# Thirty-one turns for thirty-two experts: which expert gets a turn is read from a table while the kernel runs

## The chip, the cores and the metric

The kernel runs on one core of one Trainium2 chip. The metric is the device time of one execution in microseconds (us), taken as the median of several runs. The core's engines work side by side, each through its own list of instructions: PE (matrix products), DVE (elementwise work and reductions), ACT (ScalarE), POOL (GpSimd) and SP (SyncE, which here issues most of the DMA transfers).

## The reference

The input x has 256 tokens of 1024 numbers. Everything is float32. Three layers follow one another:

- a block with a gated causal convolution over the tokens, a projection, and a residual;
- an expert layer: a router picks for each token one of 4 groups and in it the best 2 of 8 experts, and each token's row goes through its two experts;
- a multi-head latent attention layer and a block-wise attention layer, each with a gate, an output projection and a layer norm.

The expert layer is what matters here. With h the normalised tokens:

```
grp    = argmax(h @ w_rg + b_rg)                      # one of 4 groups
v, i   = top_k((h @ w_re + b_re)[grp's 8 experts], 2)
gate   = softmax(group logits)[grp] * softmax(v)
expert = grp * 8 + i                                  # 2 of 32 experts per token
out[token] += gate * (silu(xb @ w_gate[e]) * (xb @ w_up[e])) @ w_down[e]
```

An expert's three weights are 1024x512, 1024x512 and 512x1024: 2.097 MB each.

## The kernel before

**The weights** come as 2 MB pieces in one fixed list, made by `pieces()` (lines 83 to 131): the convolution block's, then three for each of the 32 experts (part 0 gate, part 1 up, part 2 down), then those of the attention layers. For the experts the list goes gate e+1, up e+1, down e, so a turn's down weight comes behind the next turn's first two. Class `Weights` (line 137) issues them on SP in this order, up to 12 pieces ahead of the one in use, into a fixed rotation of buffers: `ring_a` and `ring_b` with three each, and during the expert stage four more (`c`, `d`, `d`, `f`) in memory that earlier tiles have left. SP waits at each piece until the buffer's last reader is done. Every piece has its source address in the program. The pieces of the attention layers use `ring_a` alone.

**Routing** (lines 715 to 773). DVE makes `oh1`, a 0/1 table of tokens by experts, and `G`, the gates. PE counts with a triangular matrix how many earlier tokens chose the same expert (`pp`), and DVE makes `posp` from it: the token's place with its expert, from 1, or 0. Then the pools of this part close (`ctxB.close()`), and the tiles of the expert stage take their memory.

**An expert's turn** (lines 971 to 1035). A turn holds 64 tokens (`CAP`). `group(e)` makes 0/1 matrices (`oh`) for four experts from `posp`, and `gather` multiplies the tokens, split into two rounded halves, by them: `xg`. `start` multiplies `xg` by the gate and the up weight, `hidden` and `hidden_t` make and transpose the hidden rows, and `proj_out` multiplies them by the down weight (`pys`). DVE weights the result (`yt`, line 1029), and `split` (lines 281 to 283) makes two halves `y`. Turns go in pairs: an even turn fills rows 0 to 63 of `y`'s first 512 columns and rows 64 to 127 of its second, an odd turn the other way round, so that one product per half, `scatter`, brings a pair's rows back to their tokens in four PSUM accumulators (`acc`). `scatter_matrix` makes the pair's matrix at its even turn from `oh` and `ig`, a tile with an identity and `G`. `put()` scatters the pair before at the next even turn. The turn before the last (`e == E - 2`) makes the last turn's hidden rows ahead, between the two halves of its own projection. The last pair is scattered behind the loop (lines 1127 to 1129), where the norm's squares follow (line 1142).

**An expert with more than 64 tokens** is finished at turn 20 (`OVF_AT`), under a condition on the largest place, `mxi`, that all engines read into a register: a loop over all 32 experts (`overflow`, line 886) with the places 65 to 256 in three rounds, each with its own loads of the weights.

The planner of the framework lays out each engine's list by the program's order and by when it expects things to be ready; from the end of the convolution to the end of the experts the products stay in the program's order (`pe_order`, line 194).

Of the kernel before, what the change touches and what calls it, by code (L numbers as in the profile page):

```python
# [13 lines left out]
P = 128  # L14
# [3 lines left out]
KD = 8  # L18
E = 32
FH = 512  # L20
CAP = 64
# [61 lines left out]
def pieces():  # L83

    out = []

    def add(shape, *key):
        out.append((key, shape))

    def add_ada(v):  # L90
        for h in range(2):
            add((KD, 512), "ada", v * D + h * 512)

    add_ada(1)
    add_ada(0)
    for q in range(4):
        add((KD, 512), "cwi", 256 * q)
    for v in (4, 3, 2):
        add_ada(v)
    wo_at = len(out)  # L100
    add((KD, 512), "cwo", 0)
    add_ada(5)
    add((KD, 512), "cwo", 512)
    moe_from = len(out)

    def add_moe(e, part):
        add(((KD, FH), (KD, FH), (4, D))[part], "moe", e, part)

    for e in range(E):
        if e == 0:  # L110
            add_moe(e, 0)
            add_moe(e, 1)
        if e + 1 < E:
            add_moe(e + 1, 0)
            add_moe(e + 1, 1)
        add_moe(e, 2)
    moe_to = len(out)
    add((KD, KVL + RD), "mwi", QL)
    for h in range(2):
        add((KD, 384), "mwi", 384 * h)  # L120
    add((2, 2048), "ukv", 0)
    for i in range(4):
        add((6, 384), "uq", 384 * i)
        if i % 2 == 0:
            add((KD, 512), "mwi", QL + KVL + RD + 256 * i)
    for h in range(2):
        add((KD, 512), "mwo", 512 * h)
    for w, a in (("bkv", D), ("bkv", 0), ("bkv", 512), ("bkv", D + 512), ("bwi", 0), ("bwi", D), ("bwi", 512),
                 ("bwi", D + 512), ("bwo", 0), ("bwo", 512)):
        add((KD, 512), w, a)  # L130
    return out, wo_at, moe_from, moe_to
# [5 lines left out]
class Weights:  # L137
# [14 lines left out]
    def fill(self, upto):  # L152
        while self.nload < min(upto, self.cap, len(self.src)):
            ap, shape, pool = self.src[self.nload]
            n = 1
            for s in shape:
# [27 lines left out]
def build(tc, A, out, dbg=None, stop=None):  # L184
# [34 lines left out]
    W = Weights(nc, order, 2 * (RING_A + RING_B))  # L219

    flat, at = A["wst"], 0
    for i, (key, shape) in enumerate(PIECES):
        n = 1
        for z in shape:
            n *= z
        if key[0] == "moe":
            if key[1:] == RING_D_AT:
                ring_d_from = len(W.src)
                W.pools[:0] = ["d"] * RING_D + ["f"]
            src = A["moe"][key[1], key[2]]  # L230
        else:
            if key == ("cwo", 512):
                W.cap = len(W.src)
                W.pools.insert(0, "c")
            src = flat[at:at + P * n].rearrange("(p n) -> p n", p=P)
            at += P * n
        W.add(src, shape, ring_a if i >= MOE_TO else None)
# [9 lines left out]
    cstp = pre.tile([P, C_N - C_SEL], F32, name="cstp")  # L247
    vec = const.tile([P, V_ROWS], F32, name="vec")
    x2 = pre.tile([P, NT, D], F32, name="x2")
# [19 lines left out]
    nc.vector.memset(zeros, 0.0)  # L269
    aff = const.tile([P, 4, KD], F32, name="aff")  # L270
    small = const.tile([P, 16], F32, name="small")
# [66 lines left out]
    nc.tensor.transpose(pv, vraw, ident)  # L338
    nc.vector.tensor_copy(vec, pv)
    nc.scalar.activation(small[:, 0:8], vec[:, V_C:V_C + 8], AF.Sigmoid)  # L340
    nc.vector.tensor_mul(small[:, 0:8], small[:, 0:8], vec[:, V_C:V_C + 8])
# [376 lines left out]
    dump("lg", lg)  # L718
    posp = rt.tile([P, NT, E], F32, name="posp")
    G = rt.tile([P, NT, E], F32, name="G")  # L720
    r1 = pre.tile([P, NT, 16], F32, name="r1")
# [43 lines left out]
    nc.vector.tensor_add(oh1, oh1, oh2)  # L765
    pp = psA.tile([P, NT, E], F32, name="pp", tag="adc")
    mm(pp[:, 0, :], tri, oh1[:, 0, :], True, True)
    mm(pp[:, 1, :], ones, oh1[:, 0, :], True, False)
    mm(pp[:, 1, :], tri, oh1[:, 1, :], False, True)
    nc.vector.scalar_tensor_tensor(posp, pp, 1.0, oh1, op0=OP.add, op1=OP.mult)  # L770
    rest_of_rows(1)
    dump("posp", posp)
    dump("G", G)
# [112 lines left out]
    def overflow():  # L886

        with tc.For_i(0, E, 1) as e:
            pc = mo.tile([P, NT], F32, name="pc", tag="pc")
            gc = mo.tile([P, NT], F32, name="gc", tag="gc")  # L890
# [4 lines left out]
            def part(n, k, c=0):  # L895
                wt = mo.tile([P, 512], F32, name="wo", tag="yh1")
                q = (D * k + c) if n == 2 else 512 * k
                nc.gpsimd.dma_start(wt, A["moe"][bass.ds(e, 1), n, :, q:q + 512].rearrange("o p n -> p (o n)"))
                return wt

            so = mo.tile([P, CAP], F32, name="so", tag="so")
            xg = mo.tile([P, KD, CAP], F32, name="xgo", tag="yl0")
            for r in range(1, T // CAP):
                nc.vector.tensor_scalar(so, slot64, float(CAP * r), None, op0=OP.add)
# [45 lines left out]
    for q in range(4):  # L950
        gather(*nxt, range(2 * q, 2 * q + 2), 4 * CAP, acc[q // 2][q % 2])

    ig = mo.tile([P, P + 4 * E], F32R, name="ig")
    nc.scalar.copy(ig[:, 2 * E:2 * E + P], ident)
# [15 lines left out]

    for e in range(E):
        if e == OVF_AT:
            put()
        if e == OVF_AT:
            W.cap = 1 << 30
            rv = nc.values_load(mxi[0:1, 0:1], min_val=0, max_val=T)
            with tc.If(rv > CAP):
# [17 lines left out]
        if hn is None:  # L995
            hid = hidden(pgu)
            pgu = None
        if e + 1 < E:
            pgu = pme.tile([P, 512], F32, name="pgu", tag="pgu")
# [3 lines left out]
        if e == 1:  # L1003
            most_slots(mxi)
        wu = W.get() if e + 1 < E else None
        if e % 2 == 0:
            if e != OVF_AT and e:
                put()
            se, gs = scatter_matrix(oh, e)
            start(e + 1, xg, 1, pgu, wu)  # L1010
            if e % 4 == 2 and e + 2 < E:
                del oh, xg
                oh, xg = group(e + 2)
                for q in range(4):
                    gather(oh, xg, range(2 * q, 2 * q + 2), 4 * CAP)
            y = [[mo.tile([P, 512], F32R, name=f"y{q}{j}", tag=f"y{q}{j}") for q in "hl"] for j in range(2)]
        elif wu is not None:
            start(e + 1, xg, 1, pgu, wu)
        del wu
        w = W.get()  # L1020
        if e == E - 2:
            hid = hidden(pgu)
        pys = proj_out(hT, e % 2, lambda c, o: w[:, c, o:o + 512], ahead if e == E - 2 else None)
        hT = w = None
# [7 lines left out]
        del pys, yt  # L1032
        if e % 2:
            done = (se, y)
            del se, y, gs
# [384 lines left out]
    xh, xl = big("xh", F32R), big("xl", F32R)  # L1420
    to_channels((0, 1), x2, vec[:, V_FIN:V_FIN + 8], None, xh, xl)
    fg = rows(A["final_g"].unsqueeze(0))
# [23 lines left out]
    def latent_q(i):  # L1446
        pq = chunk_t(KD, xh, xl)
        a, v = scaled_split(cqh[:, i, :], cql[:, i, :], pq, vec[:, V_QN + i:V_QN + i + 1])
        nc.scalar.activation(sqq[:, i, :], pq, AF.Square)
# [8 lines left out]
    for k in range(2):  # L1458
        pt = ps.tile([P, T], F32, name="ptc", tag="pt", bufs=2)
        for t in range(NT):  # L1460
            nc.tensor.transpose(pt[:, P * t:P * t + P], ckn[:, t, P * k:P * k + P], ident)
        scaled_split(ckh[:, k, :], ckl[:, k, :], pt, vec[:, V_KN + k:V_KN + k + 1])

# [250 lines left out]
```

## Time and profile before

| | |
|---|---|
| median of 3 runs | 935.23 us (932.19 to 936.95) |
| the profiled execution, its own time | 931.65 us |
| its span, from the first instruction to the last | 930.0 us |
| PE busy | 871.4 us, 94% of the span |
| DVE busy | 516.4 us, 56% |
| ACT busy | 362.2 us, 39% |
| mean granted TensorE clock | 0.986 |
| bytes moved by DMA | 289.44 MB, mean 311 GB/s |

Shares of busy time are means over stages with different limits, and a busy PE is one with a product under way, at whatever rate. The stages in the order of time: convolution block to about 170 us, routing to about 187, experts to about 629, attention layers to the end.

### The profile page before, as it was taken

How to read it: one execution, taken by the hardware profiler on the slowest of the kernel's cores; microseconds unless marked ns; L12 is line 12 of the kernel's file. 1: busy time of each engine (PE TensorE's matmuls, PEld its weight loads, DVE VectorE, ACT ScalarE, POOL GpSimd, SP SyncE). 2: the span in 40 equal slices, each digit the busy share in tenths (PEclk: the TensorE clock that was granted, in tenths of full speed). 3: DMA queues.
4: the chain of work that ended last, by engine and by line, in shares of the span. 5: the costliest groups of instructions: out<-in, count | busy, mean ns of one | idle time of the engine just before them, and what ended most of it. 6: DMA issues, size and time to landing. Idle time of an engine off the chain costs nothing. (4 is left out here: it accounts for less than half of the span.)

```text
span 930.0 us, 15479 instructions
## 1 busy us (share of the span) xinstructions
PE 871.4 (94%) x6249; PEld 611.3 (66%) x6249; DVE 516.4 (56%) x1255; ACT 362.2 (39%) x794; POOL 39.7 (4%) x50
## 2 busy tenths in 40 slices
PE   4899889899999999999799999789999999999996
PEld 1598456666555565656365565448998876988975
DVE  2699876523334333433223343247778867868876
ACT  1445555522112121212112121127776646545761
POOL 0000010000000000000000000001110000210112
PEclk9899999999999999999989999999999999999999
DMA  9995887799999999999999999995433423624211
GB/s 370 411 397 205 337 351 292 295 375 426 427 425 427 427 425 428 426 427 426 427 425 427 426 427 427 427 395 206 164 139 123 181 101 137 261 91 182 91 47 45
DMA packets 23580, 289.44 MB, mean 311 GB/s; under 512 B 2736, under 2 KB 3408, under 8 KB 6096
## 3 DMA queue, kind: packets, MB, share of 16 engines
q1 hardware_dynamic: 21872, 282.29, 73.4%
q10 hardware_dynamic: 1632, 6.11, 1.9%
q8 instruction: 51, 0.84, 0.4%
q14 instruction: 25, 0.20, 0.1%
HBM read 287.34 MB, written 1.05 MB: 310 GB/s over the span
## 5 line engine op out<-in xcount | busy, mean ns | idle before, releaser
L195 PE MATMUL pgu<-w,xg 128*64 128x256 f32 x2048 | 233.5, 381 | 4.0 <-DMA w<-in_moe 4.0
L195 PEld LDWEIGHTS pgu<-w,xg 128*64 128x64 f32 x2048 | 145.7, 137 | 89.9 <-issue 20.7
L195 PE MATMUL pys<-w,hTe 128*64 128x512 f32 x512 | 116.1, 595 | 5.4 <-DMA w<-in_moe 2.6
L283 DVE TENSOR_TENSOR sl<-w,sh 128x1024 fp32r<-128x1024 f32 (+2 forms) x82 | 95.6, 1173 | 18.8 <-ACT sh L282 17.7
L282 ACT CAST sh<-w 128x1024 fp32r<-128x1024 f32 (+2 forms) x82 | 81.3, 998 | 51.1 <-PE pj L195 47.5
L1029 DVE SCALAR_TENSOR_TENSOR yt<-pys,gs,g2b 64x512 f32<-64x512 f32 x64 | 48.0, 750 | 87.2 <-PE pys L195 86.1
L282 ACT CAST yh<-yt 64x512 fp32r<-64x512 f32 x64 | 39.5, 616 | 138.8 <-DVE yt L1029 134.7
L195 PE MATMUL pj<-xh,sh 128*128 128x256 f32 x304 | 86.6, 285 | 0.0
L195 PE MATMUL pj<-xl,sh 128*128 128x256 f32 x304 | 85.6, 282 | 0.0
L195 PE MATMUL pj<-xh,sl 128*128 128x256 f32 x304 | 85.4, 281 | 0.0
L195 PEld LDWEIGHTS pys<-w,hTe 128*64 128x64 f32 x512 | 36.2, 137 | 66.0 <-issue 54.5
L863 DVE TENSOR_TENSOR hid<-pgu,hid 128x256 f32<-128x256 f32 x32 | 13.6, 424 | 98.6 <-ACT hid L862 98.6
L862 ACT ACTIVATE hid<-pgu 128x256 f32<-128x256 f32 x32 | 12.3, 383 | 120.9 <-PE pgu L195 114.8
L195 PEld LDWEIGHTS pj<-xl,sh 128*128 128x128 f32 x304 | 57.1, 188 | 1.8 <-issue 1.7
L195 PEld LDWEIGHTS pj<-xh,sh 128*128 128x128 f32 x304 | 57.1, 188 | 1.7 <-issue 1.6
L195 PEld LDWEIGHTS pj<-xh,sl 128*128 128x128 f32 x304 | 57.1, 188 | 0.8 <-issue 0.8
L414 DVE SCALAR_TENSOR_TENSOR y<-up,wdw,y 128x256 f32<-128x256 f32 x120 | 52.5, 484 | 0.1
L283 DVE TENSOR_TENSOR yl<-yt,yh 64x512 fp32r<-64x512 f32 x64 | 43.9, 686 | 2.0
L282 ACT CAST wh<-w 128x512 fp32r<-128x512 f32 x48 | 29.1, 619 | 28.9 <-PE pu L195 21.3
L195 PE MATMUL pu<-hh,wh 128*128 128x256 f32 x128 | 36.7, 287 | 2.7 <-ACT wh L282 2.7
L283 DVE TENSOR_TENSOR wl<-w,wh 128x512 fp32r<-128x512 f32 x48 | 32.3, 684 | 11.9 <-ACT wh L282 11.1
L871 DVE COPY hTe<-pth 128x256 f32<-128x256 f32 x32 | 13.6, 424 | 43.5 <-PE pth L201 38.8
(344 smaller groups left out, 1565.4 us busy)
## 6 DMA issues: line engine op xcount, KB each, us to landing
w<-in_moe SPq DMA_DIRECT2D x95, 2048.0 KB, 32.1
w<-in_wst SPq DMA_DIRECT2D x32, 2048.0 KB, 9.0
w<-in_wst SPq DMA_DIRECT2D x5, 1152.0 KB, 5.1
w<-in_wst SPq DMA_DIRECT2D x2, 1536.0 KB, 11.1
wb<-in_wbd ACTq DMA_DIRECT2D x4, 512.0 KB, 6.8
w<-in_wst SPq DMA_DIRECT2D x2, 1024.0 KB, 22.4
w<-in_moe SPq DMA_DIRECT2D x4, 512.0 KB, 31.4
x<-in_x SPq DMA_DIRECT2D x1, 1024.0 KB, 11.4
```

Source lines behind the costliest of these rows:

```text
L195: ins = nc.tensor.matmul(o, l, r, start=start, stop=stop)
L282: a = nc.scalar.copy(hi, src)
L283: return a, (eng or nc.vector).tensor_sub(lo, src, hi.bitcast(F32))
L414: nc.vector.scalar_tensor_tensor(y[:, m, :], u, wdw[:, m, k:k + 1], y[:, m, :], op0=OP.mult, op1=OP.add)
L862: nc.scalar.activation(hid, pgu[:, 0:256], AF.Silu)
L863: nc.vector.tensor_mul(hid, pgu[:, 256:512], hid)
L871: nc.vector.tensor_copy(hT, pt.rearrange("p (q j s) -> p q j s", q=2, j=2))
L1029: nc.vector.scalar_tensor_tensor(yt[r, :], pys[r, :], gs[r, e % 2:e % 2 + 1], g2b[r, 512 * j:512 * j + 512], op0=OP.mult, op1=OP.mult)
```

## The change

The loop over experts has 31 turns. The first four are experts 0 to 3 as before. For the others a small table `eidx` says which expert a turn has: the first expert from 4 on without a token (`low`) is left out, and those behind it move up by one. If all have tokens, `low` is 31, and expert 31's places are raised by 64, so that they are all done by the overflow loop, which has a fourth round and takes its experts' numbers from the table. The pieces of turns 4 to 30 take their address from a register that SP loads from the table. After the first four experts' matrices are made, the columns of `posp` and `G` are shifted in the same way. With 31 turns the last one has no partner, and the other half of `y` is filled with zeros. To make room, `vec` moves to a pool that closes early, and its last 16 columns are kept in `vecl`.

```diff
+NS = E - 1
+FIXED = 4
@@ pieces(), and the loop over the turns: NS in the place of E
-    for e in range(E):
+    for e in range(NS):
...
@@ Weights.fill
             ap, shape, pool = self.src[self.nload]
+            if callable(ap):
+                ap = ap()
@@ build
+    slot_expert = {}
+    def expert_weights(i, n):
+        if i not in slot_expert:
+            slot_expert.clear()
+            slot_expert[i] = nc.values_load(eidx[0:1, i:i + 1], engines=[mybir.EngineType.SP], min_val=i, max_val=i + 1,
+                                            skip_runtime_bounds_check_because="an index and a comparison's result")
+        return A["moe"][bass.ds(slot_expert[i], 1), n].rearrange("o p n -> p (o n)")
...
-            src = A["moe"][key[1], key[2]]
+            src = A["moe"][key[1], key[2]] if key[1] < FIXED else (lambda e=key[1], n=key[2]: expert_weights(e, n))
...
-    vec = const.tile([P, V_ROWS], F32, name="vec")
+    vec = pre.tile([P, V_ROWS], F32, name="vec")
+    vecl = const.tile([P, V_ROWS - V_QN], F32, name="vecl")
...
+    nc.vector.tensor_copy(vecl, pv[:, V_QN:])
...
+    turns = rt.tile([P, 2, E], F32, name="turns")
+    eidx = rt.tile([1, E], I32, name="eidx")
...
-    pp = psA.tile([P, NT, E], F32, name="pp", tag="adc")
+    pp = psA.tile([P, NT + 1, E], F32, name="pp", tag="adc")
...
+    mm(pp[:, 2, :], ones, oh1[:, 0, :], True, False)
+    mm(pp[:, 2, :], ones, oh1[:, 1, :], False, True)
-    nc.vector.scalar_tensor_tensor(posp, pp, 1.0, oh1, op0=OP.add, op1=OP.mult)
+    nc.vector.scalar_tensor_tensor(posp, pp[:, 0:NT, :], 1.0, oh1, op0=OP.add, op1=OP.mult)
     rest_of_rows(1)
+    late, gone = turns[:, 0, :], turns[:, 1, :]
+    low = r1[:, 0, 14:15]
+    nc.vector.tensor_scalar(late, pp[:, 2, :], 0.5, 64.0, op0=OP.is_gt, op1=OP.mult)
+    nc.vector.tensor_add(late, late, i32)
+    nc.vector.tensor_reduce(out=low, in_=late[:, FIXED:], op=OP.min, axis=AX.X)
+    nc.vector.tensor_scalar(low, low, float(E - 1), None, op0=OP.min)
+    nc.vector.tensor_scalar(late, i32, low, None, op0=OP.is_ge)
+    nc.vector.tensor_scalar(gone, i32, low, None, op0=OP.is_equal)
+    nc.vector.tensor_add(eidx[:, 0:NS], late[0:1, 0:NS], i32[0:1, 0:NS])
+    nc.vector.tensor_copy(eidx[:, NS:], low[0:1, :])
@@ overflow
+            ex = nc.values_load(eidx[0:1, bass.ds(e, 1)], engines=[mybir.EngineType.Pool], min_val=0, max_val=E - 1,
...
-            for r in range(1, T // CAP):
+            for r in range(1, T // CAP + 1):
@@ behind the gather of the first four experts
+    drop = mo.tile([P, NT, 2], F32, name="drop")
+    for c in (posp, G):
+        d = mo.tile([P, NT, E], F32, name="d", tag="so")
+        nc.vector.tensor_tensor(out=d, in0=c, in1=gone.unsqueeze(1).to_broadcast([P, NT, E]), op=OP.mult)
+        nc.vector.reduce_sum(drop[:, :, 0:1], d, axis=AX.X)
+        d = d[:, :, 0:NS]
+        nc.vector.tensor_sub(d, c[:, :, 1:], c[:, :, 0:NS])
+        nc.vector.tensor_tensor(out=d, in0=d, in1=late[:, 0:NS].unsqueeze(1).to_broadcast([P, NT, NS]), op=OP.mult)
+        nc.vector.tensor_add(c[:, :, 0:NS], c[:, :, 0:NS], d)
+        if c is posp:
+            nc.vector.tensor_scalar(drop[:, :, 1:2], drop[:, :, 0:1], 0.5, float(CAP), op0=OP.is_gt, op1=OP.mult)
+            nc.vector.tensor_add(c[:, :, NS:], drop[:, :, 0:1], drop[:, :, 1:2])
+        else:
+            nc.vector.tensor_copy(c[:, :, NS:], drop[:, :, 0:1])
@@ the loop over the turns, an even turn
+            if wu is not None:
+                start(e + 1, xg, 1, pgu, wu)
...
+            if e + 1 == NS:
+                for j in range(2):
+                    for q in range(2):
+                        r = slice(64 - 64 * j, 128 - 64 * j)
+                        nc.vector.tensor_scalar(y[j][q][r, :], g2b[r, 0:512], 0.0, None, op0=OP.mult)
...
-        if e % 2:
+        if e % 2 or e + 1 == NS:
             done = (se, y)
```

## Rows read from the trace of the kernel before

**Rows 1.** The page's slices, 23.25 us each: DMA share in tenths, and GB/s.

```profile
DMA  9995887799999999999999999995433423624211
GB/s 370 411 397 205 337 351 292 295 375 426 427 425 427 427 425 428 426 427 426 427 425 427 426 427 427 427 395 206 164 139 123 181 101 137 261 91 182 91 47 45
```

**Rows 2.** Four turns: stretch, length, busy time by engine, clock, DMA share, GB/s.

```profile
237.53:290.10 52.57, 51.98 (x383) 30.83 (x381) 19.48 (x42) 10.93 (x22) 0.00 (x0) 1.00 1.01 427
```

**Rows 3.** DMA issues of the page: count, KB each, median us from issue to landing.

```profile
w<-in_moe SPq DMA_DIRECT2D x95, 2048.0 KB, 32.1
```

**Rows 4.** Waits of PE, 540 to 625 us: total, times, longest.

```profile
PE pgu L195 <- DMA w<-in_moe: 4.0, 5, 1.2
PE pys L195 <- DMA w<-in_moe: 2.6, 2, 1.3
```

**Rows 5.** Timeline, end of the stage: start, length, instruction, idle before it.

```profile
599.36 3.65 PE L195 MATMUL pys<-w,hTe 128*64 128x512 f32 x16 [1.31 <-DMA w<-in_moe]
...
609.97 0.36 PE L195 MATMUL pt<-ig,oh 128*128 128x192 f32 x2
...
615.33 1.94 PE L195 MATMUL pys<-w,hTe 128*64 128x512 f32 x8 [1.33 <-DMA w<-in_moe]
...
619.89 1.52 DVE L1029 SCALAR_TENSOR_TENSOR yt<-pys,gs,g2b 64x512 f32<-64x512 f32 x2
...
620.02 3.65 PE L195 MATMUL pys<-w,hTe 128*64 128x512 f32 x16 [0.53 <-DVE hTe L871]
...
623.73 1.53 DVE L1029 SCALAR_TENSOR_TENSOR yt<-pys,gs,g2b 64x512 f32<-64x512 f32 x2 [0.76 <-PE pys L195]
...
625.17 0.73 PE L195 MATMUL acc<-yh,se 128*128 128x512 f32 x2 [1.49 <-ACT yh L282]
625.29 0.68 DVE L283 TENSOR_TENSOR yl<-yt,yh 64x512 fp32r<-64x512 f32 x1
...
626.94 0.59 ACT L1142 ACTIVATE junk<-acc 128x512 f32<-128x512 f32 x1
```

**Rows 6.** Timeline of routing's end, PE and DVE.

```profile
179.12 0.39 PE L195 MATMUL pp<-oh,ones 128*128 128x32 f32 x2
...
179.34 0.39 PE L195 MATMUL pp<-oh,cstp 128*128 128x32 f32 x2
...
179.77 0.23 DVE L770 SCALAR_TENSOR_TENSOR posp<-pp,oh 128x64 f32<-128x64 f32 x1 [0.81 <-PE pp L195]
...
182.03 0.58 DVE L797 TENSOR_SCALAR oh<-cst,posp 128x64 fp32r<-128x64 f32 x3 [2.04 <-PE pw L195]
```

**Rows 7.** Timeline of SP: two issues at the start of the stage.

```profile
190.79 0.33 SPq L166 DMA_DIRECT2D w<-in_moe  x1
...
194.25 0.33 SPq L166 DMA_DIRECT2D w<-in_moe  x1
```

**Rows 8.** Timeline: DVE's first gathered tile, PE's first weight product.

```profile
185.07 0.54 DVE L814 TENSOR_SCALAR xg<-acc,aff,modc 128x256 f32<-128x256 f32 x1 [1.24 <-ACT xg L817]
...
187.08 0.65 PE L195 MATMUL pgu<-w,xg 128*64 128x256 f32 x4
```

**Rows 9.** Line 976, SP reads mxi: ns min/median/max, first and last start.

```profile
L976 SPq TENSOR_LOAD <-mxi x1: 479/479/479, 461.0 to 461.0; - x1
L976 SPq FUSED_REGOPS  x1: 191/191/191, 462.0 to 462.0; - x1
```

**Rows 10.** Line 977, the jump over the overflow code, on PE.

```profile
L977 PEldq COMPARE_BRANCH  x1: 6027/6027/6027, 459.1 to 459.1; - x1
```

**Rows 11.** Timeline of turn 20: the result's DVE step, the scatter's last product.

```profile
455.45 1.53 DVE L1029 SCALAR_TENSOR_TENSOR yt<-pys,gs,g2b 64x512 f32<-64x512 f32 x2 [6.62 <-PE pys L195]
...
459.49 0.40 PE L195 MATMUL acc<-yl,se 128*128 128x512 f32 x1
```

**Rows 12.** Stretches, columns as in Rows 2; the granted clock is third from the end.

```profile
455.00:460.00 5.00, 3.04 (x10) 1.35 (x8) 3.52 (x6) 1.93 (x4) 0.00 (x0) 1.00 1.02 436
627.00:630.00 3.00, 2.84 (x5) 1.50 (x5) 1.37 (x4) 2.77 (x10) 0.55 (x1) 0.51 0.87 368
```

More of the change, by code (lines that the diff above doesn't have):

```diff
@@ L112, in pieces @@
             add_moe(e, 1)
-        if e + 1 < E:
+        if e + 1 < NS:
             add_moe(e + 1, 0)
@@ L269, in build @@
     nc.vector.memset(zeros, 0.0)
-    aff = const.tile([P, 4, KD], F32, name="aff")
+    aff = const.tile([P, 2, KD], F32, name="aff")
     small = const.tile([P, 16], F32, name="small")
@@ L888, in overflow @@
         with tc.For_i(0, E, 1) as e:
+            ex = nc.values_load(eidx[0:1, bass.ds(e, 1)], engines=[mybir.EngineType.Pool], min_val=0, max_val=E - 1,
+                                skip_runtime_bounds_check_because="an index of an expert")
             pc = mo.tile([P, NT], F32, name="pc", tag="pc")
@@ L897, in part @@
                 q = (D * k + c) if n == 2 else 512 * k
-                nc.gpsimd.dma_start(wt, A["moe"][bass.ds(e, 1), n, :, q:q + 512].rearrange("o p n -> p (o n)"))
+                nc.gpsimd.dma_start(wt, A["moe"][bass.ds(ex, 1), n, :, q:q + 512].rearrange("o p n -> p (o n)"))
                 return wt
@@ L951, in build @@
         gather(*nxt, range(2 * q, 2 * q + 2), 4 * CAP, acc[q // 2][q % 2])
+    drop = mo.tile([P, NT, 2], F32, name="drop")
[12 more added lines that the diff above has]
+            nc.vector.tensor_copy(c[:, :, NS:], drop[:, :, 0:1])
+        del d
     ig = mo.tile([P, P + 4 * E], F32R, name="ig")
@@ L969, in put @@
             scatter(done, t, e < 4, False)
-    for e in range(E):
+    for e in range(NS):
         if e == OVF_AT:
@@ L975, in build @@
             W.cap = 1 << 30
-            rv = nc.values_load(mxi[0:1, 0:1], min_val=0, max_val=T)
+            rv = nc.values_load(mxi[0:1, 0:1], min_val=0, max_val=T + CAP)
             with tc.If(rv > CAP):
@@ L997, in build @@
             pgu = None
-        if e + 1 < E:
+        if e + 1 < NS:
             pgu = pme.tile([P, 512], F32, name="pgu", tag="pgu")
@@ L1004, in build @@
             most_slots(mxi)
-        wu = W.get() if e + 1 < E else None
+        wu = W.get() if e + 1 < NS else None
         if e % 2 == 0:
@@ L1009, in build @@
             se, gs = scatter_matrix(oh, e)
-            start(e + 1, xg, 1, pgu, wu)
-            if e % 4 == 2 and e + 2 < E:
+            if wu is not None:
+                start(e + 1, xg, 1, pgu, wu)
+            if e % 4 == 2 and e + 2 < NS:
                 del oh, xg
@@ L1020, in build @@
         w = W.get()
-        if e == E - 2:
+        if e == NS - 2:
             hid = hidden(pgu)
-        pys = proj_out(hT, e % 2, lambda c, o: w[:, c, o:o + 512], ahead if e == E - 2 else None)
+        pys = proj_out(hT, e % 2, lambda c, o: w[:, c, o:o + 512], ahead if e == NS - 2 else None)
         hT = w = None
@@ L1420, in build @@
     xh, xl = big("xh", F32R), big("xl", F32R)
-    to_channels((0, 1), x2, vec[:, V_FIN:V_FIN + 8], None, xh, xl)
+    to_channels((0, 1), x2, vecl[:, V_FIN - V_QN:V_FIN - V_QN + 8], None, xh, xl)
     fg = rows(A["final_g"].unsqueeze(0))
@@ L1447, in latent_q @@
         pq = chunk_t(KD, xh, xl)
-        a, v = scaled_split(cqh[:, i, :], cql[:, i, :], pq, vec[:, V_QN + i:V_QN + i + 1])
+        a, v = scaled_split(cqh[:, i, :], cql[:, i, :], pq, vecl[:, i:i + 1])
         nc.scalar.activation(sqq[:, i, :], pq, AF.Square)
@@ L1461, in build @@
             nc.tensor.transpose(pt[:, P * t:P * t + P], ckn[:, t, P * k:P * k + P], ident)
-        scaled_split(ckh[:, k, :], ckl[:, k, :], pt, vec[:, V_KN + k:V_KN + k + 1])
+        scaled_split(ckh[:, k, :], ckl[:, k, :], pt, vecl[:, V_KN - V_QN + k:V_KN - V_QN + k + 1])
     kc = [big("kc", shape=(8, T)) for i in range(2)]
```

## The prediction

> **What bounds the kernel now.** I read the page's slices first [rows 1]: from the tenth of the 40 slices to the 26th the DMA engines are full (digit 9) at about 426 GB/s. That is the expert stage, up to about 620 us. Its 32 turns are one expert each, and a turn needs three pieces of 2.097 MB: 6.29 MB / 427 GB/s = 14.73 us of transfer. The busy shares call PE full too, so I then asked for PE's own pace away from the ends of the stage [rows 2]: four turns, with everything that they share, take 52.57 us, 13.14 us a turn, without a wait for a weight. PE is therefore 1.6 us a turn faster than the weights, and lives on what the ring held ahead: a piece lands 32.1 us after its issue, six and a half transfers deep [rows 3]. The lead runs out late, and the waits of PE between 540 and 625 us [rows 4] show it: five waits on a gate or up weight (4.0 us), two on a down weight (2.6 us), and hardly anything else. So the wait that ends last in this stage is the transfer: pieces land 4.9 us apart, and the end of the stage hangs on the last four. Behind this stage the list of waits has no product of PE that waits for a weight, so what the stage gains reaches the end of the kernel.
>
> **The sum's base.** The profiled execution took 931.65 us (span 930.0), 3.6 us under the median of the runs, 935.23. I work out a difference against the profile and apply it to the median.
>
> **Removed: one turn.** The reference's router, on the inputs as drawn, gives expert 26 none of the 512 places, and the fullest expert 59, under the 64 that a turn holds. So the change drops expert 26, the 31 others keep their turns, and neither kernel enters the overflow loop. Three pieces go: 3 x 4.91 = 14.73 us of transfer. PE loses a turn as well, but that is the looser of the two. Because the list of pieces ends (gate 30, up 30, down 29, down 30), down 29 is the same piece in the same place as before; it landed when PE began on it, at 599.36 [rows 5]. I build the new end of the stage from that point.
>
> **Added before the stage, on the path.** Two more products of 128x32 into pp (179.12 and 179.34 are two such, 0.22 us apart; I take 0.23 [rows 6]) stand before posp and before the products into pw. The one-hot tiles wait for the last pw, since they lie in its pool's memory, so PE's start slips by 2 x 0.23 = **0.46 us**. Does the transfer slip as well? The queue ran dry there: the next piece is issued at 190.79, when the first gate weight has been read [rows 7]. So yes.
>
> **Added before the stage, covered.** Eight small DVE steps make the list of turns. A DVE step of 128x64 takes 0.23 us [rows 6], and I allow 0.26 from start to start: at most 2.1 us. DVE sits idle for 2.04 us between posp and the first one-hot, waiting for pw [rows 6]. Covered but for 0.1; without the cover, 2.1 us. The release of the pool that one more weight buffer waits for comes under the same cover, and the queue still holds earlier pieces. The thirteen steps that shift posp and G come behind the one-hots: 13 x 0.26 = 3.4 us at most, from 183.4 to 186.8, plus 0.46. DVE's first xg would move from 185.07 to 187.3 and be done at 187.8; PE's first weight product starts at 187.08 + 0.46 = 187.54 and comes to that second eighth of its 3.7 us at 188.0 [rows 8]. Covered, just. If ScalarE's copies of the shifted G are queued ahead of its own xg, PE waits: up to 1.5 us. I take 0. The copy of 16 more columns of vec at the start is one step of at most 0.23 us, beside ScalarE's sigmoid: 0.
>
> **The table on SP's queue.** From turn 4 on, 54 times a turn's number is read into SP's register. The trace has such a read: 0.48 us, and a register step of 0.19 [rows 9]. A turn puts 2 x 0.48, some five register steps and three issues of 0.33 on SP: 2.9 us of 14.73. What queues behind a read is the next issue, and behind that only transfers, which have a queue 32 us deep. The first reads come where it is shallow: issues stand at 190.79 and 194.25 [rows 7], the piece of 190.79 keeps the engines busy until 195.7 at the earliest, and a read plus a step makes the second 194.9. Cost 0; if the depth were gone, 54 x 0.67 = 36 us. The stall at turn 20, where PE takes 6.03 us to jump over the overflow code [rows 10], stays, and PE's lead pays it in both kernels.
>
> **The end of the stage, where time is given back.** Before, the last turn was the second of its pair, and its projection started 0.5 us after the one ahead of it [rows 5]. Now turn 30 stands alone, and the scatter of pair 28/29 and its own scatter matrix come in PE's order between the two projections. From 599.36 + 0.46 = 599.82:
> - projection of 29, with the transposes of 30 in its middle, to the DVE step on its result: before 615.33 to 619.89, 4.56 [rows 5]; 604.38.
> - that step to the end of the scatter: at turn 20 the same order stands, 455.45 to 459.89, 4.44 [rows 11]; 608.82.
> - scatter matrix, 0.36 (row 609.97); 609.18.
> - projection of 30: 620.02 to 623.73, 3.71; 612.89.
> - four DVE steps that zero the other half of y. Nearest row: 64x512 into the same type, two operands, 0.68 (row 625.29); 2.7 us at most. They fit between the scatter and 612.89 unless they queue behind the scatter matrix's results: 0 to 1.3; I take 0.3. So 613.2 against 623.73: **10.55 us earlier**.
> - The last scatter starts with the output half 1, which an even turn finishes second. Before, the first scatter product started 1.44 us after the DVE step and the first square 3.21 us after it [rows 5]; half of the DVE step (0.76 of 1.53) and one split (0.68) come in between now. 0 to 1.4; I take **1.0**.
>
> Net 10.55 - 1.0 = 9.55, say 9.5: of the 14.7 removed, 0.5 goes to the start, 4.7 to the end. Profile 922.1; median **925.7 us**. The three buffers of the next stage's first pieces come free earlier than before (their last experts' pieces are 27, 28 and 29 instead of 29 to 31), so nothing new is late there.
>
> **Rivals.**
> - *The clock falls in the new tail.* Between the two projections PE now idles and scatters in short bursts. [...] Against it: at turn 20 the same idle and scatter kept 1.00 from 455 to 460 us. [...]
> - *The tail is free.* The piece of turn 30 lands by 605; if the planner found room for scatter and scatter matrix inside projection 29, all but 0.46 of the transfer's gain would stay: 14.3, 920.9. Against: the products are kept in the order of the program.
> - *Given back elsewhere.* Pools and lists differ (vec, aff, the tables), and the planner may order the first 180 us or ScalarE's queue anew. The bounds above add 1.5 + 2.1 + 1.0 + 0.4 us: gain 4.5, 930.7, no change that can be measured.
> - *Slower: SP sets the pace.* If a read of a turn's number can't run ahead, because it or the address waits for transfers in flight, the queue empties at each. The restart at 190.79 shows the price: about 2 us of engine time. 54 x 2.0 = 108 us against 9.5: 1,024. It decides from 0.18 us lost per read. Against: the number is a tile written once at 182, and the read of the trace waits for no transfer.
> - *It doesn't do what it says*: were no expert empty, all 32 x 4 overflow rounds would load 6.29 MB each, 1.9 ms more. The counts exclude it for these inputs.
>
> **How the numbers follow.** Forecast 0.68 (its own range 921 to 929), clock 0.12, free tail 0.05, given back 0.08, SP 0.05, overflow 0.02. About 0.5%, 4.7 us, is what a measurement tells from no change: faster means below 930.5. All of the forecast but its edge, the free tail and most of the clock case lie there: 0.80. Same 0.13: that edge, the rest of the clock case, and "given back". Slower 0.07. The range of 8 in 10 takes the bounds of the start (0 to 1.5 us), the zeroing (0 to 1.3) and the spread of the medians (2 us): 920 to 931.
>
> **What would show it.** Right: DMA full to about 605 instead of 620; down 29 read at about 599.8; a scatter and a scatter matrix between the last two projections; the first one-hot at about 182.5; 31 x 3 transfers from the expert weights; no DMA gap after the reads. Wrong: any DMA slice under 9 inside the stage (SP), a granted clock of 0.5 around 609 to 613, a start of the first weight product after 188.5, or a stage after the experts that takes longer than before.

## The result, and the profile after

The changed kernel takes 924.06 us (median of 4 runs, 923.13 to 927.19) against 934.64 us of the kernel before in the same comparison (4 runs, 932.19 to 936.95): a ratio of 0.9893, 95% interval 0.9857 to 0.9929, by which it is 10.0 us less (6.6 to 13.4); the two medians lie 10.6 apart. A second comparison on another chip gave 0.9895 (0.9878 to 0.9912). The prediction was 925.7 us.

The two profiled executions lie closer together than the medians: 931.65 and 923.4 us (spans 930.0 and 921.8). The pair shows 8.2 us, because that of before is 3.0 us under its median and that of after only 0.7. Below I follow these 8.2 us row by row.

The slices of the page after, 23.05 us each (DMA share in tenths, GB/s), beside [rows 1]:

```profile
DMA  9995887789999999999999999974432433624211
GB/s 360 421 407 208 316 350 295 299 349 425 429 426 426 428 424 429 424 429 427 427 421 429 427 426 427 423 293 177 183 140 96 183 109 134 261 98 177 93 47 46
```

The transfer is as full as before, at 421 to 429 GB/s (425 to 428 before), and the full stretch ends one slice earlier: the 27th has 293 GB/s where before it had 395. The list of issues, of waits of PE from 540 to 625 us (total, times, longest) and of SP's reads of the table (ns min/median/max, first and last start), beside [rows 3, 4, 9]:

```profile
w<-in_moe SPq DMA_DIRECT2D x92, 2048.0 KB, 31.9
```

```profile
PE acc L199 <- ACT yh L297: 3.4, 2, 1.8
PE pgu L199 <- DMA w<-in_moe: 2.6, 4, 1.2
PE pys L199 <- DMA w<-in_moe: 1.3, 1, 1.3
```

```profile
L231 SPq TENSOR_LOAD <-eidx x54: 262/270/478, 192.1 to 561.8; - x54
```

Three transfers fewer, each in flight 31.9 us in the median (32.1 before). PE still waits for weights at the end of the stage, 3.9 us instead of 6.6, so the transfer still bounds it. What is new is 3.4 us of waiting for ACT ahead of two scatters. A read of the table takes 0.27 us, not the 0.48 of [rows 9].

The timeline of after (start, length, instruction, idle time before it), for [rows 5 to 8]: the end of routing, the first weight product, SP's first issues by the table, and the end of the stage.

```profile
179.89 0.61 PE L199 MATMUL pp<-oh,ones 128*128 128x32 f32 x4
180.54 0.23 DVE L790 SCALAR_TENSOR_TENSOR posp<-pp,oh 128x64 f32<-128x64 f32 x1 [1.26 <-PE pp L199]
180.68 0.18 DVE L796 TENSOR_SCALAR turns<-pp 128x32 f32<-128x32 f32 x1
...
181.93 0.13 DVE L803 CAST eidx<-r 1x1 int32<-1x1 f32 x1
182.80 1.39 DVE L829 TENSOR_SCALAR oh<-cst,posp 128x64 fp32r<-128x64 f32 x8 [0.74 <-PE pw L199]
...
187.98 1.30 PE L199 MATMUL pgu<-w,xg 128*64 128x256 f32 x10
...
191.69 3.81 SPq L170 DMA_DIRECT2D w<-in_moe  x2
...
600.70 1.94 PE L199 MATMUL pys<-w,hTe 128*64 128x512 f32 x8 [1.35 <-DMA w<-in_moe]
...
605.26 1.52 DVE L1087 SCALAR_TENSOR_TENSOR yt<-pys,gs,g2b 64x512 f32<-64x512 f32 x2
...
606.70 0.50 PE L199 MATMUL acc<-yh,se 128*128 128x512 f32 x1 [1.83 <-ACT yh L297]
...
608.29 0.79 PE L199 MATMUL acc<-yl,se 128*128 128x512 f32 x1
...
610.57 0.58 PE L199 MATMUL pt<-ig,oh 128*128 128x192 f32 x2
610.82 0.42 DVE L1074 TENSOR_SCALAR yl<-g2b 64x512 fp32r<-64x512 f32 x1
611.08 3.75 PE L199 MATMUL pys<-w,hTe 128*64 128x512 f32 x16
...
614.88 1.53 DVE L1087 SCALAR_TENSOR_TENSOR yt<-pys,gs,g2b 64x512 f32<-64x512 f32 x2 [0.36 <-PE pys L199]
...
616.39 1.46 PE L199 MATMUL acc<-yh,se 128*128 128x512 f32 x4 [1.55 <-ACT yh L297]
...
618.80 0.60 ACT L1200 ACTIVATE junk<-acc 128x512 f32<-128x512 f32 x1 [1.73 <-PE acc L199]
...
624.29 1.06 PE L1257 MATMUL pt<-cst,x 128*128 128x128 f32 x8 [1.28 <-DVE x L1210]
```

The last result step moves from 623.73 to 614.88, the first square from 626.94 to 618.80 (8.1 us earlier), and the span ends 8.2 earlier. Behind the first square nothing changes (303.0 us to the end, 303.1 before). Stretches of the same trace (length, busy time by engine, granted clock, DMA share, GB/s), beside [rows 12]:

```profile
237.00:290.00 53.00, 52.41 (x388) 31.04 (x386) 19.86 (x43) 11.27 (x23) 0.00 (x0) 1.00 1.01 427
...
604.00:608.00 4.00, 1.82 (x9) 0.48 (x3) 2.98 (x5) 1.23 (x2) 0.00 (x0) 0.99 1.04 425
608.00:611.00 3.00, 3.00 (x9) 2.17 (x7) 1.65 (x5) 0.00 (x0) 0.00 (x0) 0.50 0.92 390
611.00:616.00 5.00, 3.83 (x17) 1.14 (x16) 3.21 (x8) 2.63 (x6) 0.00 (x0) 0.97 0.57 217
...
618.00:621.00 3.00, 3.00 (x7) 1.74 (x6) 0.00 (x0) 2.13 (x6) 0.00 (x0) 0.53 0.17 68
```

Transfers whose address comes from a register run at the same 427 GB/s as those of [rows 2]. And the granted clock is at half, 0.50, from 608 to 611 us, in the scatter that now stands between the last two projections. That stretch is new. The one from 618 to 621 (0.53) is not: it stands at the first square, as the one of the kernel before does (0.51 from 627 to 630 [rows 12]), and behind it PE still waits 1.28 us for DVE.

### The profile page after: what moved, and what is told of

The parts are those of the page before. It is cut to its first block, busy times and chain, and to the rows that moved or that the text cites. A ratio compares the mean times of both kernels' runs of the same rounds, so it can differ in the third digit from the quotient of the medians.

```text
span 921.8 us, 15557 instructions
## 1 busy us (share of the span) xinstructions
PE 862.7 (94%) x6171; PEld 606.6 (66%) x6171; DVE 517.4 (56%) x1275; ACT 361.1 (39%) x791; POOL 39.6 (4%) x51
## 5 line engine op out<-in xcount | busy, mean ns | idle before, releaser
L199 PE MATMUL pgu<-w,xg 128*64 128x256 f32 x1984 | 226.1, 381 | 2.9 <-DMA w<-in_moe 2.9
L199 PEld LDWEIGHTS pgu<-w,xg 128*64 128x64 f32 x1984 | 140.6, 137 | 86.4 <-issue 18.7
L199 PE MATMUL pys<-w,hTe 128*64 128x512 f32 x496 | 112.5, 595 | 3.5 <-DVE xg L846 2.1
L298 DVE TENSOR_TENSOR wl<-w,wh 128x512 fp32r<-128x512 f32 x48 | 32.3, 683 | 12.3 <-ACT wh L297 11.6
L199 PE MATMUL pu<-hh,wl 128*128 128x256 f32 x128 | 37.1, 290 | 0.0
## 6 DMA issues: line engine op xcount, KB each, us to landing
w<-in_moe SPq DMA_DIRECT2D x92, 2048.0 KB, 31.9
```

Of the source, the lines that this page charges most:

```text
L199: ins = nc.tensor.matmul(o, l, r, start=start, stop=stop)
L298: return a, (eng or nc.vector).tensor_sub(lo, src, hi.bitcast(F32))
```

## The experiments

Each ratio is against the kernel before, run beside it on the same chip; e1 to e4, e5 to e8 and e9 to e11 shared one each.

### Is the gain the transfer, or the turn?

**e3_idle_pieces**: the changed kernel, which still transfers expert 26's three pieces, with nothing reading them. Cut to its core:

```diff
+        if e == 26:
+            for n in range(3):
+                add((KD, FH), "moe", 26, n, "idle")
...
+        if e == 26:
+            for n in range(3):
+                W.get()
```

> The changed kernel, but the dropped expert's three pieces are still transferred ahead of turn 27's and read by nobody: 32 turns of transfer, 31 turns of PE. Theory (transfers): the whole 14.7 us come back, 938 to 939 us, and so 4 us over the kernel before, since the lone last turn stays. Rival (PE's turn was what went): 924 to 926 us, as the changed kernel.

Measured: 939.3 us, 1.0072 (1.0055 to 1.0089), 6.7 us slower than before (5.1 to 8.3). The timeline: PE's weight products behind its longest wait and those of a later turn, the projection of turn 29, the scatter between the last two projections, and the first square.

```profile
561.23 5.89 PE L202 MATMUL pgu<-w,xg 128*64 128x256 f32 x32 [15.23 <-DMA w<-in_moe]
...
610.14 3.67 PE L202 MATMUL pgu<-w,xg 128*64 128x256 f32 x32 [0.85 <-DMA w<-in_moe]
...
615.16 1.94 PE L202 MATMUL pys<-w,hTe 128*64 128x512 f32 x8 [1.35 <-DMA w<-in_moe]
...
621.16 0.50 PE L202 MATMUL acc<-yh,se 128*128 128x512 f32 x1 [1.83 <-ACT yh L300]
...
632.78 0.60 ACT L1206 ACTIVATE junk<-acc 128x512 f32<-128x512 f32 x1 [2.49 <-PE acc L202]
```

PE has one turn fewer and waits for the three pieces instead, 15.23 us at one place. The products behind that wait are slower by 2.2 us, but this doesn't reach the end: PE waits for weights again, and its projection at 615.16 stands where the kernel before has the one on the piece at the same place in the list, 615.33 [rows 5]. So the turn that PE is spared is worth nothing as long as the transfer stays, and without the transfer's part there is no gain. What is lost lies behind that projection: in the two profiles it takes 17.6 us from there to the first square, where the kernel before takes 11.6, and 0.6 more follow. The prediction had 4.7 for the new end. Part of the rest is the half clock, which here lies on the last scatter (0.50 from 631 to 634 us; a product of it at 630.41 takes 0.63 us, those of the scatter at 621.16 take 0.39 to 0.50).

**e5_less_transfer**: the reverse, the kernel before with all 32 turns and 7/8 of three pieces not transferred. Cut to its core:

```diff
+            if PIECES[self.nload][0][:2] == ("moe", 26):
+                self.nc.sync.dma_start(t[:, 0:512], ap[:, 0:512])
+                self.nc.gpsimd.memset(t[:, 512:n], 0.0)
```

> The kernel before, with all its 32 turns, but of the three pieces of expert 26 only the first eighth (512 of 4,096 columns) is transferred, and GpSimd writes zeros to the rest. 7/8 x 14.73 = 12.9 us of transfer go, no work of TensorE goes. My theory (the transfer bounds the end of the stage, TensorE lives 6.6 us behind it: its waits of 4.0 + 2.6 us for weights between 540 and 625 us): the gain is what TensorE waited, 6 to 7 us against the kernel before, and the waits for weights at the end of the stage are gone. Rival one (TensorE sets the pace of the stage by itself): within 1 us of the kernel before. Rival two (nothing but the transfer counts, TensorE's work for a turn is free): 12 to 13 us faster.

Measured: 926.22 us, 0.9918 (0.9903 to 0.9934), 7.7 us faster (6.2 to 9.1). Of PE's waits for weights from 187 to 625 us one of 0.2 us is left:

```profile
PE pgu L201 <- DMA w<-in_moe: 0.2, 1, 0.2
```

Of 12.9 us of transfer some 7.7 come through; then PE's own work ends last. Both rivals are out: PE alone would have given nothing, the transfer alone 12 to 13. The second bound is about 7 us behind the first. A change that takes away more transfer than that and no work of PE is cut off there.

### Does the table cost anything?

**e2_reads_32_turns**: the kernel before, with the 56 reads and register addresses from a table that holds 0 to 31. Cut to its core (the tile `aff` is also made smaller, as in the changed kernel):

```diff
-            src = A["moe"][key[1], key[2]]
+            src = A["moe"][key[1], key[2]] if key[1] < 4 else (lambda e=key[1], n=key[2]: expert_weights(e, n))
```

> The kernel before, 32 turns, with nothing of the change but the reads: the sources of turns 4 to 31 come from a table that holds 0 to 31, so 56 reads on SP. Theory: as before within 1.5 us (933 to 936). Rival (the reads cost the gain its missing part, some 4 to 5 us): 938 us or more.

Measured: 933.26 us, 1.0006 (0.9993 to 1.0018). Free: the rival in which SP sets the pace is refuted to within some 1.7 us.

**e1_fixed_addresses**: the changed kernel with expert 26 skipped by number.

```diff
-            src = A["moe"][key[1], key[2]] if key[1] < FIXED else (lambda e=key[1], n=key[2]: expert_weights(e, n))
+            src = A["moe"][key[1] + (key[1] >= 26), key[2]]
```

> The changed kernel with the sources of all pieces fixed when it is built (turn e takes expert e, from turn 26 on expert e + 1): no read of the table on SP; the table and the shift of the columns stay. Theory (transfers set the stage, SP's reads are hidden behind its queue): within 1.5 us of the changed kernel, 922.5 to 925.5 us, and the down weight of turn 29 is read at 600.7 as there. Rival (the reads hold the transfers up): faster by more than 3 us, the first weights of the shallow queue earlier.

Measured: 926.45 us, 0.9934 (0.9913 to 0.9954): nothing gained, rather 2 to 4 us lost against the changed kernel's 0.9893 and 0.9895, which no theory expected. In its profile the first product of routing already stands at 180.94 us, 2.2 later than in a second profile of the changed kernel (178.78, e8 below), with PE's instructions in the same order until there; from that product to the first weight product both take 8.8 us. That places 1.7 to 2.2 us ahead of anything the edit touches. More than half of it arises in one early stretch, where the granted clock differs; e1, then the changed kernel:

```profile
20.00:26.00 6.00, 5.67 (x24) 1.85 (x24) 2.21 (x6) 0.00 (x0) 0.00 (x0) 0.50 1.01 429
```

```profile
20.00:26.00 6.00, 5.61 (x30) 2.19 (x28) 2.58 (x7) 0.46 (x1) 0.00 (x0) 1.00 0.99 419
```

Ahead of it e1 is 0.4 us earlier than the changed kernel (at 19 us), behind it 0.65 later (at 36). Nor does the clock belong to the program: the changed kernel's own executions with a mean granted clock of 0.981 and 0.980 took 924.7 and 927.2 us, and the one execution of e1 with 0.985 took 923.3, as the changed kernel's two with 0.985 did (923.1 and 923.4). What sets the clock of an execution is open. That reading the table costs nothing stands on e2.

### What does the bookkeeping ahead of the stage cost?

**e6_fixed_bookkeeping**: the changed kernel without the two products, the list, the shift and the reads of the table. **e8_changed_again**: the changed kernel as it is, beside it.

```diff
-    mm(pp[:, 2, :], ones, oh1[:, 0, :], True, False)
-    mm(pp[:, 2, :], ones, oh1[:, 1, :], False, True)
...
-    nc.vector.tensor_scalar(late, pp[:, 2, :], 0.5, 64.0, op0=OP.is_gt, op1=OP.mult)
...
+    nc.vector.tensor_copy(eidx, i32[0:1, :])
...
+        nc.vector.tensor_copy(d, c[:, :, 27:])
+        nc.vector.tensor_copy(c[:, :, 26:NS], d)
+        nc.vector.memset(c[:, :, NS:], 0.0)
```

> The changed kernel with the list of turns settled when the kernel is built (expert 26 is left out by its number): the two more products into pp, the eight steps that make the list, the eleven steps of the shift but for two copies and the reads of the table are gone; the last turn's columns are zero. My theory: the two products are all that stands on the path ahead of the stage (0.46 by the prediction, 0.90 as the trace after has it), so the start of the first weight product comes back to 187.1 to 187.5 us and the kernel is 0.5 to 1.3 us faster than the changed one. Rival (the slip of the start is a different order of the work before the stage and not these steps): the start stays at 187.9 or later and the time within 0.4 us.

> The changed kernel as it is, once more, beside the three others on the same chip, so that differences of less than 1 us can be told. All theories: a ratio of 0.987 to 0.991, that is 922 to 925 us.

Measured: e6 924.75 us, 0.9902 (0.9885 to 0.9919); e8 923.64 us, 0.9895 (0.9878 to 0.9912). No gain, so by the time the rival is right, but not by its reason. Timelines of the two, routing's first product into pp and the first weight product; e6, then e8:

```profile
179.22 0.41 PE L199 MATMUL pp<-oh,cstp 128*128 128x32 f32 x2 [0.59 <-DVE oh L782]
...
187.56 1.73 PE L199 MATMUL pgu<-w,xg 128*64 128x256 f32 x14
```

```profile
178.78 0.41 PE L199 MATMUL pp<-oh,cstp 128*128 128x32 f32 x2 [0.59 <-DVE oh L783]
...
187.57 1.73 PE L199 MATMUL pgu<-w,xg 128*64 128x256 f32 x14
```

From the one to the other it is 8.34 us without the bookkeeping and 8.79 with it: the two products account for 0.45 us, and the other steps for nothing that shows. But executions of one program differ as much before that point (178.78 here, 179.20 in the first profile of the changed kernel). My theory's error was to expect 0.45 us in the medians. In e6's profile, besides, a half-clock stretch falls where it costs time, of which more below.

### Does the half clock in the new tail cost time?

**e7_warm_products**: the changed kernel with two more products, read by nobody, between the projection of turn 29 and the scatter.

```diff
+            if e + 1 == NS:
+                pw = pme.tile([P, 512], F32, name="pw", tag="pgu")
+                for i in range(2):
+                    mm(pw, ident, g2b[:, 0:512], True, True)
```

> The changed kernel with two more products of 128x512, read by nobody, between the projection of turn 29 and the scatter of pair 28/29. My theory: the half clock granted from 608 to 611 us follows the idle time of TensorE ahead of the scatter; with the two products in it the scatter and the scatter matrix are granted the full clock and the last projection starts 0.5 to 1 us earlier: 0.3 to 0.9 us faster than the changed kernel. Rival (the clock there follows the short bursts of the scatter, not the idle time ahead of them): the scatter's products stay at 0.6 to 0.8 us and the time is the same or up to 0.8 us longer by the two products.

Measured: 923.74 us, 0.9887 (0.9868 to 0.9906), e8 beside it 923.64. Its timeline, and stretches in the columns used above; then the last of them in the changed kernel; then one stretch of e6 and one of e3:

```profile
601.02 1.94 PE L199 MATMUL pys<-w,hTe 128*64 128x512 f32 x8 [1.32 <-DMA w<-in_moe]
...
605.12 1.98 PE L199 MATMUL pw<-g2b,cst 128*128 128x512 f32 x4
...
605.58 1.52 DVE L1092 SCALAR_TENSOR_TENSOR yt<-pys,gs,g2b 64x512 f32<-64x512 f32 x2
...
609.85 0.36 PE L199 MATMUL pt<-ig,oh 128*128 128x192 f32 x2
610.14 3.65 PE L199 MATMUL pys<-w,hTe 128*64 128x512 f32 x16
```

```profile
608.00:611.00 3.00, 3.00 (x13) 1.75 (x15) 2.06 (x5) 0.69 (x2) 0.00 (x0) 1.00 0.98 415
626.00:628.00 2.00, 2.00 (x11) 1.97 (x11) 1.38 (x4) 1.13 (x3) 0.00 (x0) 0.50 1.04 254
```

```profile
626.00:628.00 2.00, 1.62 (x14) 1.45 (x13) 2.00 (x6) 1.63 (x4) 0.00 (x0) 1.00 0.59 223
```

```profile
626.00:628.00 2.00, 2.00 (x10) 1.97 (x11) 1.52 (x4) 0.98 (x3) 0.00 (x0) 0.50 1.04 274
```

```profile
621.00:625.00 4.00, 3.36 (x14) 2.03 (x16) 3.02 (x8) 1.16 (x3) 0.00 (x0) 1.00 0.90 368
```

With the idle time filled, the scatter has the full clock, 1.00, and the two projections start 9.12 us apart (601.02, 610.14) instead of 10.38 (600.70, 611.08). This fits my theory, but one profile doesn't prove it: in e3 the same scatter behind the same wait of 1.83 us has the full clock with nothing filled in.

The 1.26 us don't last. In the changed kernel the second stretch of half clock lies at the first square, where PE ends with time to spare (1.28 us of waiting for DVE behind it). In e7 it comes later, from 626 to 628, on products of the next block, where PE is busy throughout. From the projection of turn 29 to the last product of that block it is 50.0 us in the changed kernel (650.7) and 50.4 in e7 (651.4). That the products brought this on isn't shown: e6, which has the half clock in the scatter as the changed kernel does, has it from 626 to 628 as well, and 51.2 us for the same way (600.04 to 651.2). So the half clock in the scatter costs about 1 us, on top of what the kernel before had; filling the idle time took it away in e7, and the place of the next stretch, which differs from one kernel to another for reasons that stay open, gave as much back.

### A version that beats both

**e4_lone_turn_early**: the same idea with the turn without a partner taken from the end. Expert 5's place in the list of turns is left out, turn 4 stands alone, and the experts from 5 up to the one without tokens each move one turn back. The last two turns are then a pair, as in the kernel before. Cut to its core:

```diff
-NS = E - 1
+HOLE = 5
+TURNS = [e for e in range(E) if e != HOLE]
...
-    nc.vector.tensor_scalar(late, i32, low, None, op0=OP.is_ge)
+    nc.vector.tensor_scalar(early, i32, low, None, op0=OP.is_le)
...
-    nc.vector.tensor_add(eidx[:, 0:NS], late[0:1, 0:NS], i32[0:1, 0:NS])
-    nc.vector.tensor_copy(eidx[:, NS:], low[0:1, :])
+    nc.vector.tensor_copy(eidx[:, 0:HOLE], i32[0:1, 0:HOLE])
+    nc.vector.tensor_sub(eidx[:, HOLE + 1:], i32[0:1, HOLE + 1:], early[0:1, HOLE + 1:])
+    nc.vector.tensor_copy(eidx[:, HOLE:HOLE + 1], low[0:1, :])
```

> The changed kernel with the turn without a partner moved from the end to turn 4 (turn 5 is left out, the experts from 5 to the empty one move back by one turn, the last two turns are a pair again). Theory (the lone last turn gives back what its scatter and scatter matrix take between the last two projections): the end of the stage is as in the kernel before, 13.4 to 13.8 us earlier than there, 920 to 921.5 us, 3 to 5 us under the changed kernel. Rival (the gain's missing part was lost elsewhere: start, clock, the stages behind): as the changed kernel, 923 to 925 us.

Measured: 918.64 us, 0.9846 (0.9828 to 0.9864), 14.4 us faster than before and some 4.5 faster than the changed kernel. The end of its stage:

```profile
604.71 1.94 PE L201 MATMUL pys<-w,hTe 128*64 128x512 f32 x8
...
607.18 3.65 PE L201 MATMUL pys<-w,hTe 128*64 128x512 f32 x16 [0.53 <-DVE hTe L906]
610.88 1.53 DVE L1092 SCALAR_TENSOR_TENSOR yt<-pys,gs,g2b 64x512 f32<-64x512 f32 x2 [0.88 <-PE pys L201]
...
614.24 0.59 ACT L1205 ACTIVATE junk<-acc 128x512 f32<-128x512 f32 x1
```

The last two projections stand side by side, the last result step comes at 610.88 (before 623.73, after 614.88), and no product waits for a weight from 540 us on. The tail is the place where the change gave time back; PE itself is now what ends last.

In e4's profile the stop at turn 20 had become longer: from the transposes ahead of it to those behind it 31.7 us (437.84 to 469.50), 26.1 before (447.92 to 474.01). **e9_early_again** repeats e4; **e10_early_jump_16** and **e11_early_jump_12** have the jump over the overflow code at another turn, and nothing else:

```diff
-OVF_AT = 20
+OVF_AT = 16
```

> The kernel with the lone turn early (expert 5's place), once more, beside two kernels that differ from it only in the turn that the jump over the overflow code stands at. Theory: TensorE's own work sets its end, and the stop at turn 20 was longer in its profile (437.8 to 469.5 us between two turns, 31.7 against 26.1 us before) by the place of its instructions, which is the same in each execution: again 917 to 920 us, and again some 31 us. Rival: the longer stop was an accident of one execution: about 26 us here.

> The kernel with the lone turn early, and the jump over the overflow code at turn 16 instead of 20. Theory: if the stop is as long as in the kernel before (26 us between the two turns around it), TensorE ends the stage up to 5.6 us earlier than with the longer stop, until the transfer bounds it again: its last piece landed some 1 to 2 us ahead of its use, so 0.5 to 2 us faster than the kernel with the jump at turn 20: 916 to 918.5 us. Rival: the longer stop comes along with the jump wherever it stands: within 0.5 us of it.

> The kernel with the lone turn early, and the jump over the overflow code at turn 12. Theory as with turn 16: 916 to 918.5 us where the stop is 26 us long; the lead of the transfers is smaller at turn 12 (TensorE is 1.6 us a turn faster than they), and a stop there can be caught up over more turns, so no wait for a weight is to come back at the end of the stage but by the transfer's own bound. Rival: within 0.5 us of the kernel with the jump at turn 20.

Measured: 918.51 us, 0.9837 (0.982 to 0.9853); 917.68 us, 0.983 (0.9813 to 0.9848); 920.77 us, 0.9867 (0.9848 to 0.9887). The gain of e4 is repeated. The stop is 29.6, 29.9 and 30.3 us long in these three, and each has the same second gap behind the jump; the two gaps of e9, then the second of e10:

```profile
456.69 1.20 PE L201 MATMUL acc<-xh,dg 128*128 128x512 f32 x2 [5.59 <-PEq L1034]
...
462.10 0.80 PE L201 MATMUL acc<-xh,dg 128*128 128x512 f32 x1 [2.08 <-issue]
```

```profile
407.39 0.63 PE L201 MATMUL acc<-xh,dg 128*128 128x512 f32 x1 [2.86 <-issue]
```

PE stands still for 2 to 3 us while it waits for nothing that the profile shows. So e4's long stop was no accident of one execution, and it comes along with the jump at turns 20, 16 and 12 alike. Moving it to turn 16 gains nothing that can be told from no change; at turn 12 each execution (919.74 at best) is slower than the slowest of e9 (919.60), though at a lower granted clock on the mean (0.980 to 0.983 against 0.981 to 0.988). Why the changed kernel has no such second gap is open.

## Why the prediction was right

It was right in its reason: the transfer is what ends last, three pieces of it go (e3, e5), and about a third of their 14.73 us is given back at the start and in the new order of the end. Step by step, as differences of the two profiled executions; together they make the 8.2 us:

| step | predicted | measured |
|---|---|---|
| routing's first product into pp | 0 | +0.32 (178.88 to 179.20) |
| from it to the first weight product | +0.46 | +0.58 (8.20 to 8.78) |
| from there to the projection of turn 29 | 0 | +0.44 (412.28 to 412.72) |
| from there to the last result step | -11.0 | -10.2 (24.37 to 14.18) |
| from there to the first square | +1.0 | +0.7 (3.21 to 3.92) |
| all behind | 0 | 0 (303.1 to 303.0) |
| sum | -9.5 | -8.2 |

**The start.** The two products cost 0.45 us (e6 against e8), as worked out. The other 0.13 of 0.58 is in e6 as well (8.34 against 8.20 before), without the list and without the shift; its cause stays open. The 0.32 ahead of them is no cost of the change: the same program's second profile has 178.78. The transfer slipped along, as I argued: SP's issues of [rows 7] moved by 0.90, as the first weight product did. I gave nothing for the next 412 us, and they came out 0.44 longer; in e8 it is 0.24 (187.57 to 600.09), in e6 0.20. With 90 pieces that is 0.1% or less of the transfer, and nothing here tells a cause.

**Covered steps.** The eight steps run from 180.68 to 182.06; the wait for pw behind them is still 0.74 us, so they are free, as said. The shift ended at 187.47; ScalarE's copies of the shifted G stand at 187.61 between two of its xg, and PE's first weight product follows the gathers without an idle time: 0. The nearest row, 0.23 us a step, held: they took 0.13 to 0.24.

**The mis-sized term: from turn 29's result to the end of the scatter.** I took 4.44 us from turn 20 [rows 11]; it was 5.31 (605.26 to 610.57). The other terms of the end came as worked out: the projection of 29 4.56 (4.56), the scatter matrix 0.51 (0.36), the projection of 30 3.80 (3.71), and the zeros, which lie between 609.53 and 611.24, 0 (0.3). The 0.87 are the half clock: six of the scatter's eight products took 0.60 to 0.79 us, where at turn 20 all eight took 0.39 to 0.50. Its full price is 1.04, for e7, at the full clock, takes 4.27 for the same way (605.58 to 609.85); my 4.44 was 0.17 too long, since it ran to the end of the last product, and the next one starts before that. So my rival of the falling clock came true in part. I had weighed it by turn 20, whose same stretch kept 1.00 [rows 12], and so missed that the clock fell here; and I had looked for the fall at the last projection, which by my estimate, 3.71 us at half the rate (0.51 in [rows 12]), would have taken 7.4; it began at 611.08, with the clock back at 0.97 on the mean, and took 3.75. With the idle time filled e7 has 1.00 instead of 0.50, but turn 20 and e3 kept 1.00 behind a like wait (1.50 and 1.83 us, 1.83 in the changed kernel), so the wait by itself doesn't tell whether the clock falls, and what makes it fall is not shown.

**The tail.** 0.7 instead of 1.0. The last scatter's eight products ran as four of the high and four of the low part, and not in twos as before; what that is worth isn't shown. e4, which leaves the arrangement out, is 4.5 us faster, near the 4.7 that the prediction gave back to the end; but since its stop at turn 20 is longer too, that is no clean price.

**The level.** The gain by the two ratios, 10.0 and 9.8 us, lies nearer to my 9.5 than the row-by-row 8.2 do: executions of the changed kernel alone lie between 923.13 and 927.19. A prediction from one profile can't be better than that.

**The signs I named.** Down 29 was read at 600.70 (599.8 named), the first one-hot at 182.80 (182.5), the weights' transfers are 3 fewer, and the first weight product came before 188.5. The DMA engines stayed full to 608 and not to 605. Of the signs against me one showed, the half clock around 609.

**A sum that was wrong.** The rival in which SP sets the pace should have read 925.7 + 108 = 1,034 us, not 1,024. Nothing hangs on it: e2 puts the cost of the reads at 0.6 us (-0.7 to 1.7).

## What to carry to other kernels

Where a stage is bound by its transfers, price a removed piece of work by the transfer, then ask at once how far behind the second bound is: here 14.7 us of transfer went, 7 to 8 would have come through without PE's turn (e5), 10 did with the turn at the end, and 14.4 with the odd turn put where PE still has a lead to gain (e4). Here an odd remainder of a loop over pairs belonged early in such a stage and not at its end, where each microsecond of order is on the path. And a half-clock stretch of PE cost 1.0 us here on the scatter, which the last projection stands behind, and nothing that shows at the first square, where PE then waits 1.28 us for DVE.

## What the runs showed of the hardware

- A read of a number from SBUF into SP's register took 0.27 us (median of 54; 0.48 the first), and transfers with an address from it ran at 427 GB/s, as with fixed addresses; 56 reads cost 0.06% (-0.07 to 0.18%).
- The same scatter behind a wait of about 1.5 to 1.8 us had the full clock at turn 20 of the kernel before (455 to 460 us) and in e3 (621 to 625), and half of it from 608 to 611 after: one row at one place doesn't tell the clock at another.
- Behind the jump over the overflow code the kernels with the early odd turn show a second stop of PE, 2.1 to 2.9 us, in four of four profiles; the kernel before and the changed one show none.
